# Decoder trunk on one core: adaLN halves, first up tiles and rotary tables placed elsewhere

## The chip, the cores and the metric

The kernel runs on one core of one Trainium2 chip. The metric is device time in microseconds (us) of one execution; each kernel is run several times and the median is compared. In the text PE is TensorE, DVE is VectorE, ACT is ScalarE, POOL is GpSimd and SP is SyncE. SP computes nothing here and issues most of the loads; POOL issues most of the saves and some loads.

## The reference

One layer of a decoder trunk on x of 512 tokens x 2048 channels, in float32, conditioned by a vector c through adaLN:

```python
def reference(x, c, positions, w_in, w_a, w_b, w_o, w_ada, b_ada, g_mix, g_ffn,
              w_up, conv_w, conv_b, w_down, g_final):
    c_act = jax.nn.silu(c)
    for layer in range(DEPTH):
        mod = c_act @ w_ada[layer] + b_ada[layer]
        sh1, sc1, gt1, sh2, sc2, gt2 = jnp.split(mod[:, None, :], N_MOD, axis=-1)
        h = rmsnorm(x, g_mix[layer]) * (1 + sc1) + sh1
        x = x + (1 + gt1) * mixer(h, positions, w_in[layer], w_a[layer], w_b[layer], w_o[layer])
        h = rmsnorm(x, g_ffn[layer]) * (1 + sc2) + sh2
        x = x + (1 + gt2) * conv_ffn(h, w_up[layer], conv_w[layer], conv_b[layer], w_down[layer])
    return rmsnorm(x, g_final)
```

The mixer is one input projection, a stick-breaking attention of 8 heads, a sparse attention of 8 heads with rotary positions and an indexer that picks 128 keys, two projections w_a and w_b that are merged by gates, and an output projection w_o. conv_ffn is an up-projection to 2 x 5632 channels (w_up), a causal convolution of width 3 along the tokens, silu of one half times the other, and a down-projection (w_down).

## The kernel before

**Products.** Float32 products are made of three fast ones: each operand is split into a high part and a remainder, and `mm3` (L178 to L180) multiplies high by high, high by low and low by high. Weights come into one of eight `raw` buffers of 512 KB (`load`, L154, issued by SP), ACT copies the high part to `wh` (L168) and DVE subtracts it to get `wl` (L170), in `parts`. There are three rooms for `wh` and `wl`, so weights are ready at most two products ahead of PE, and L168 waits until PE has left a room. Activations are split by `split`: ACT L197, DVE L199.

**Units.** The input projection, w_o and the up-projection are computed in `unit`: a Strassen scheme (in Winograd's form) with seven products in place of eight, each of 24 steps of 128x256. Four weight tiles a11, a21, a22, a12 are loaded, DVE makes the sums and differences of them that the products need (L268, L272, L306, L310, in place in `raw`), and others of products' results (L276, L308, L309, L312, L314). `sp` holds some of these results: L308 writes the second half of a buffer whose first half L276 wrote and reads r2, in which PE then starts the next product (T3): so PE waits for L308. A unit calls `between` at two places, where other work is put beside it. The right operands (forms of the activations) lie in `F`, a tag of 62 slots of 256 KB; 56 of them hold the forms in the up-projection, which leaves six.

**What lies beside them.** mod, the adaLN vector, is c_act times w_ada, and is made without PE: a half is a tile of w_ada, loaded into `raw` (L702, `ada_load`), times c, summed along the row by DVE (L711, `some_ada`); 96 of these halves are spread over the stages by calls of the two. They are taken in the order in which they were asked for. The last of them lie before in the units of w_o, one or two a unit, and must be done before the second norm. The rotary tables are made by a generator that runs beside the first units (`rope_tables`); ACT writes the sines (L609, L610) into a `raw` buffer of 512 KB, which is saved to memory as `rope`.

**Stages in order of time.** c and the first norm; 31 units of the input projection (w_x); indexer and values; stick-breaking heads; sparse heads with w_a beside them; w_b with the gates (L1092, L1093), which yields the operands of w_o (`y` are the heads' outputs, split at L1080); eight units of w_o, the last of them with the second norm inside (`late`, `norm_late`: its square root is L1148); the first three pairs of tiles of the up-projection, computed plainly while the second norm's operands come (`plain`, `ups`); 41 up units, each followed by its convolution, `finish` (ACT L1210 and L1217, DVE L1211, L1212 and L1219, saved to `yd` at L1220), which takes the two `w` buffers; and the down-projection (`strassen_down`) with the last norm.

**The first three pairs.** They are computed before the forms are all there. Before, the six tiles are saved to memory (`ud`) and read back one by one beside the seventh and later up units by `finish_first` (loads at L1337 into a slot, ACT L1330, DVE L1333), as the generator is run at the start of a unit.

**What sets the order.** The program is written as one sequence, and a scheduler places each instruction on its engine's queue, by what it depends on and by its place in the program. `behind` keeps an instruction after another. Within one engine, and within SP's queue of loads, the order is then fixed: what stands first must go first.

Of the kernel before, what the change touches and what calls it, by code (L numbers as in the profile page):

```python
# [36 lines left out]
NU = 3  # L37
# [39 lines left out]
def block_kernel(ctx: ExitStack, tc: tile.TileContext, A: dict, out: bass.AP):  # L77
# [164 lines left out]
    def unit(src, f, between=lambda *_: None, late=None):  # L242
# [16 lines left out]
        a11 = load(src[0], w)  # L259
        a21 = load(src[2], w)  # L260
        a22 = load(src[3], w)
        a12 = load(src[1], w)
        product(r1, parts(a11, w, True), "B11", True)
# [3 lines left out]
        s = t2k("raw", 8, w=w)  # L267
        last_v = tt(s, a21, a22, ALU.add)  # L268
# [280 lines left out]
    def rope_tables():  # L549
# [55 lines left out]
        for n, step in enumerate((64, 32)):  # L605
            o = t2k("raw", 8, w=1024)
            for i in range(P // step):
                at = slice(step * i, step * i + step)
                act(o[at, :S], q1[:step], AF.Sin, scale=TWO_PI)  # L609
                act(o[at, S:], q2[:step], AF.Sin, scale=TWO_PI if i % 2 else -TWO_PI)  # L610
                if i % 2:
                    yield
            save(rope_d[n], o)
# [134 lines left out]
    for u in range(1, 32):  # L748

        def between(i, *pins):  # L750
            if not i:
                ada_load()
            with behind(*pins):
                next(work)
                if i:
                    some_ada()

        pair = unit(A["w_x"][u - 1], f, between)
        for i, o in enumerate(pair):
            if u >= 16:  # L760
                sig = act(o, o, AF.Sigmoid)
            save(xd[2 * u + i], o)
# [114 lines left out]
    for i in range(16):  # L877
        run(fill, 2)
        run(index)
    run(fill)  # L880
# [176 lines left out]
    for hd in range(NH):  # L1057
        ada_load(2 if hd > 1 else 0)
        p, s, last = sparse_1(*pairs[hd])
        if before:  # L1060
            sparse_4(*before, y)
        if hd + 1 < NH:
            pairs.append(turned(hd + 1))
        run(fill)
        with behind(last):
            some_ada(2 if hd > 1 else 0)
        ada_load(2 if hd else 0)
        last = sparse_2(p, s)
        run(fill)
        before = hd, sparse_3(p), vb[hd // 4]  # L1070
        with behind(last):
            some_ada(2 if hd else 0)
        run(fill, 2)
    sparse_4(*before, y)
# [5 lines left out]
    y = [split(o) for o in y]  # L1080
    f = []
    merged = []
    for j in range(KT):
        t = t2k("w", 2)
        save(t, td[j])
        g = fetch(xd[33 + 2 * j])
        merged.append(g)
        ps = acc()
        w = prep(A["w_b"][j])
        for k in range(NH):  # L1090
            mm3(ps, cols(w, k), y[k], k == 0, k == NH - 1)
        tt(g, ps, g, ALU.mult)  # L1092
# [38 lines left out]
    def norm_late(c1, c2):  # L1131
# [28 lines left out]
        yield  # L1160
        tile_of(1, R)
# [15 lines left out]
    for u in range(KT // 2):  # L1177
# [6 lines left out]
        for i, c in enumerate(unit(A["w_o"][u], f, between, late)):  # L1184
# [108 lines left out]
    ud = dram("ud", 2 * NU)  # L1293
    for i, ps in enumerate(ups):
        save(ud[i], evac(ps))
# [30 lines left out]
    def finish_first():  # L1326

        def half(j, u):
            t = t2k("T", 2)
            act(t, u, AF.Identity, scale=cw[:, j, 2:3], bias=cw[:, j, 3:4])  # L1330
            for i in (1, 2):
                yield t
                stt(t[:, i:], u[:, : S - i], cw[:, j, 2 - i : 3 - i], t[:, i:], ALU.mult, ALU.add)  # L1333

        def bring(i):
            u = slot()
            nc.sync.dma_start(u, ud[i])  # L1337
            return u

        for j in range(NU):  # L1340
            u = bring(2 * j)
            yield
            yield
            for a in half(2 * j, u):
                yield
            act(a, a, AF.Silu)
            u = bring(2 * j + 1)
            yield
            yield
            for b in half(2 * j + 1, u):  # L1350
                yield
            tt(a, a, b, ALU.mult)
            save(yd[j // 2][:, j % 2 * S : (j % 2 + 1) * S], a)
            yield

    gate, first_tiles = last_gate(), finish_first()
    for j in range(NU, NJ):
        if 2 * NU <= j < 2 * NU + 2:
# [3 lines left out]
        if j >= 3 * NU:  # L1362
            run(first_tiles)
# [68 lines left out]
    def strassen_down(v, src, f, done, step=lambda i: None):  # L1432
# [12 lines left out]
        kept = []  # L1445
        for g in groups:
            a11, a21, a22 = (load(src[g, q]) for q in (0, 2, 3))
# [7 lines left out]
            kept.append(a22)  # L1455
            step(g)
# [11 lines left out]
        for i in range(2):  # L1468
            tt(c22[i], c22[i], e3[i], ALU.add)
            done((2 + i, 2 * v + 1), c22[i])  # L1470
        for g in groups:
            a12, a22 = (load(src[g, q]) for q in (1, 3))
# [3 lines left out]
            product(rc, a12, "B22", g, False)  # L1476
            step(len(groups) + g)
# [254 lines left out]
```

## Time and profile before

| what | us |
|---|---|
| median of three runs | 2738.51 |
| the three runs | 2733.37, 2738.51, 2740.41 |
| the profiled execution's own time | 2737.63 |
| its span, first to last instruction | 2735.7 |
| PE busy in it | 2677.8 |
| DVE busy | 2406.6 |
| ACT busy | 1448.4 |
| POOL busy | 315.8 |

The profile is of one execution, and busy times of engines overlap. PE's share is 98%, over 18700 matmuls; since matmuls follow each other in a pipeline, a single one lasts longer in the profile than the distance to the next. The granted clock of TensorE was 0.995 of full speed on average. DMA engines moved 202 GB/s on average. A wait is put down to the instruction or transfer that ended last before the waiting one began.

### The profile page before, as it was taken

Reading aid. Unit: us, or ns where it says so; the run is one execution under the profiler, and the core shown is the slowest. Engines: PE = TensorE matmul, PEld = TensorE weight load, DVE = VectorE, ACT = ScalarE, POOL = GpSimd, SP = SyncE. Lnnn points to the kernel's source line nnn. Section 1 sums busy time; section 2 is a strip of 40 time slices with the busy share of each in tenths; the row PEclk is TensorE's granted clock in tenths of the full one; section 3 lists DMA queues with packets and bytes.
Section 4 is the critical chain, followed back from the end, with each engine's and each line's share of the span. In section 5 each row is a group of like instructions: output and inputs, shape, how many; then the busy total and the mean of one; then the engine's idle time right before and its main releaser. Section 6 shows DMA issues by size and latency. Waiting matters only on the chain.

```text
span 2735.7 us, 47661 instructions
## 1 busy us (share of the span) xinstructions
PE 2677.8 (98%) x18700; PEld 2453.8 (90%) x18700; DVE 2406.6 (88%) x3402; ACT 1448.4 (53%) x2037; POOL 315.8 (12%) x514
## 2 busy tenths in 40 slices
PE   8999999999999999999999999999999999999998
PEld 6789999999997778889999999999999998887876
DVE  8888989999987899798878999999999997888887
ACT  4444455554446665434466555555555455546443
POOL 0000010100012211112220000000000000003011
PEclk9999999999999999999999999999999999999999
DMA  9883556666676648766864666666666436468785
GB/s 351 326 301 123 174 199 196 192 212 220 205 227 203 199 140 285 237 206 216 243 215 136 189 175 189 173 181 175 171 177 181 132 125 223 154 179 236 207 228 166
DMA packets 167853, 551.65 MB, mean 202 GB/s; under 512 B 21750, under 2 KB 22390, under 8 KB 167628
## 3 DMA queue, kind: packets, MB, share of 16 engines
q1 hardware_dynamic: 119820, 408.49, 46.4%
q0 software_dynamic: 47216, 139.73, 18.7%
q8 instruction: 147, 2.41, 0.3%
q14 instruction: 78, 0.64, 0.1%
q10 hardware_dynamic: 592, 0.39, 0.1%
HBM read 453.97 MB, written 91.14 MB: 199 GB/s over the span
## 4 chain that ended last, share of the span: by engine, by line
PE 83%; DVE 8%; DMA 4%; issue 3%; ACT 2%; SPq 0%; POOL 0%; ACTq 0%; DVEq 0%; POOLq 0%
PE att L180 13%; PE att L179 13%; PE att L178 13%; PE acc L179 12%; PE acc L180 12%; PE acc L178 12%; DVE wl L170 2%; PE acc L928 1%; DMA F<-ud 1%; ACT wh L168 1%; DMA raw<-in_w_down 1%; PE outs L179 1%; PE outs L178 1%; PE outs L180 1%; PE acc L896 1%
## 5 line engine op out<-in xcount | busy, mean ns | idle before, releaser
L168 ACT ACTIVATE wh<-raw 128x1024 fp32r<-128x1024 f32 (+1 forms) x790 | 828.8, 1055 | 945.7 <-DVE raw L272 174.9
L170 DVE TENSOR_TENSOR wl<-raw,wh 128x1024 fp32r<-128x1024 f32 (+1 forms) x790 | 953.4, 1214 | 125.3 <-ACT wh L168 117.7
L178 PE MATMUL acc<-F,wh 128*128 128x256 f32 (+1 forms) x2448 | 702.3, 287 | 9.0 <-DVE sp L308 4.3
L178 PE MATMUL att<-F,wh 128*128 128x256 f32 (+1 forms) x2448 | 704.3, 288 | 6.2 <-DVE sp L308 5.2
L180 PE MATMUL acc<-F,wl 128*128 128x256 f32 (+1 forms) x2448 | 701.5, 287 | 8.1 <-DVE wl L170 8.1
L180 PE MATMUL att<-F,wl 128*128 128x256 f32 (+1 forms) x2448 | 702.3, 287 | 4.3 <-DVE wl L170 4.3
L179 PE MATMUL att<-F,wh 128*128 128x256 f32 (+1 forms) x2448 | 701.6, 287 | 0.2 <-DVE F L199 0.2
L179 PE MATMUL acc<-F,wh 128*128 128x256 f32 (+1 forms) x2448 | 701.2, 287 | 0.1
L178 PEld LDWEIGHTS acc<-F,wh 128*128 128x128 f32 x2448 | 460.2, 188 | 21.8 <-issue 5.1
L178 PEld LDWEIGHTS att<-F,wh 128*128 128x128 f32 x2448 | 461.6, 189 | 17.4 <-issue 5.7
L180 PEld LDWEIGHTS acc<-F,wl 128*128 128x128 f32 x2448 | 460.4, 188 | 18.1 <-DVE wl L170 9.3
L180 PEld LDWEIGHTS att<-F,wl 128*128 128x128 f32 x2448 | 461.7, 189 | 13.2 <-DVE wl L170 5.0
L179 PEld LDWEIGHTS att<-F,wh 128*128 128x128 f32 x2448 | 461.7, 189 | 8.8 <-DVE F L199 0.7
L179 PEld LDWEIGHTS acc<-F,wh 128*128 128x128 f32 x2448 | 460.5, 188 | 10.1 <-DVE F L490 0.8
L178 PE MATMUL att<-wh,F 128*128 128x512 f32 x448 | 177.8, 398 | 0.2 <-ACT wh L168 0.2
L179 PE MATMUL att<-wl,F 128*128 128x512 f32 x448 | 175.3, 391 | 0.7 <-DVE wl L170 0.7
L180 PE MATMUL att<-wh,F 128*128 128x512 f32 x448 | 175.1, 391 | 0.0
L179 PE MATMUL acc<-wl,F 128*128 128x512 f32 x288 | 113.5, 394 | 4.3 <-DVE wl L170 4.3
L268 DVE TENSOR_TENSOR raw<-raw,raw 128x1024 f32<-128x1024 f32 x80 | 97.4, 1218 | 18.9 <-DMA raw<-in_w_o 14.1
L178 PE MATMUL acc<-wh,F 128*128 128x512 f32 x288 | 112.4, 393 | 0.1
L180 PE MATMUL acc<-wh,F 128*128 128x512 f32 x288 | 111.3, 391 | 0.0
L711 DVE SCALAR_TENSOR_TENSOR raw<-raw,raw 128x1024 f32<-128x1024 f32 x89 | 107.3, 1217 | 0.8 <-DMA raw<-in_w_ada 0.8
(370 smaller groups left out, 3719.9 us busy)
## 6 DMA issues: line engine op xcount, KB each, us to landing
raw<-in_w_up SPq DMA_DIRECT2D x164, 512.0 KB, 3.8
raw<-in_w_ada SPq DMA_DIRECT2D x152, 512.0 KB, 5.2
raw<-in_w_x SPq DMA_DIRECT2D x128, 512.0 KB, 4.3
raw<-in_w_down SPq DMA_DIRECT2D x104, 512.0 KB, 4.5
xd<-F POOLq DMA_DIRECT2D x64, 256.0 KB, 3.0
F<-xd POOLq DMA_DIRECT2D x64, 256.0 KB, 4.9
raw<-in_w_o SPq DMA_DIRECT2D x32, 512.0 KB, 5.5
soft<-in_w_gate SPq DMA_DIRECT2D x32, 512.0 KB, 3.9
```

What stands on the lines that cost most here:

```text
L168: pins["wh"] = act(wh, raw, AF.Copy)
L170: pins["wl"] = tt(wl, raw, wh.bitcast(F32), ALU.subtract)
L178: mm(ps, ah, bh, start=first, stop=False, skip_group_check=not check)
L179: mm(ps, ah, bl, start=False, stop=False, skip_group_check=not check)
L180: return mm(ps, al, bh, start=False, stop=last, skip_group_check=not check)
L268: last_v = tt(s, a21, a22, ALU.add)
L711: stt(w, w, 1.0, cb[half], ALU.mult, ALU.mult, accum_out=macc[:, t, half : half + 1])
L896: mm(zk, k[:, q0 : q0 + P], q[:, q0:], start=kb != 3, stop=False, skip_group_check=True)
L928: mm(o, negtri if tri else negones, i, start=False, stop=True, skip_group_check=True)
```

## The change

Seven places are edited. Line numbers in the rows are those of each kernel's own file.

1. The rotary tables are written into two slots of `F` each, in place of one `raw` buffer, and saved as two halves.
2. The adaLN halves are asked for and summed in other places: more in the 29th to 31st w_x unit, two beside the first values, three more in each of the last two sparse heads. The loop over w_o still has its calls, fewer of them, but finds nothing left.
3. The outputs of the first three sparse heads are split before the last head's end, the others after it as before.
4. The loads, the first `parts` and the first sum of w_o's first unit (`unit_head`) are written ahead of the last w_b tile's gates.
5. A square root of a constant into an unused column is written ahead of the late square root of the second norm.
6. The six first up tiles stay in their slots and are finished by `finish` just before the first, second and third up unit; the memory tensor `ud`, its saves and loads and `finish_first` are gone.
7. In `strassen_down` the loads of a group are written one group ahead.

```diff
-            o = t2k("raw", 8, w=1024)
+            o = [slot() for _ in range(2)]
...
-                act(o[at, :S], q1[:step], AF.Sin, scale=TWO_PI)
-                act(o[at, S:], q2[:step], AF.Sin, scale=TWO_PI if i % 2 else -TWO_PI)
+                act(o[0][at], q1[:step], AF.Sin, scale=TWO_PI)
+                act(o[1][at], q2[:step], AF.Sin, scale=TWO_PI if i % 2 else -TWO_PI)
...
-            save(rope_d[n], o)
+            for i in range(2):
+                save(rope_d[n][:, i * S : (i + 1) * S], o[i])
...
     for u in range(1, 32):
         def between(i, *pins):
+            free = u in (29, 30)
             if not i:
+                ada_load(2 if free else 1)
+            elif u == 29:
                 ada_load()
             with behind(*pins):
                 next(work)
-                if i:
-                    some_ada()
+                if i or u == 30:
+                    some_ada(2 if free and i else 1)
...
     for i in range(16):
+        if i in (3, 9):
+            ada_load()
         run(fill, 2)
         run(index)
+        if i in (6, 12):
+            some_ada()
...
         run(fill)
+        if hd > 5:
+            ada_load(3)
         before = hd, sparse_3(p), vb[hd // 4]
         with behind(last):
-            some_ada(2 if hd else 0)
+            some_ada((2 if hd else 0) + (3 if hd > 5 else 0))
         run(fill, 2)
+    y[:3] = [split(o) for o in y[:3]]
     sparse_4(*before, y)
...
-    y = [split(o) for o in y]
+    y[3:] = [split(o) for o in y[3:]]
...
+        if j == KT - 1:
+            head = unit_head(A["w_o"][0], KT // 2 * P)
         tt(g, ps, g, ALU.mult)
...
         with behind(*pins):
-            some_ada()
-        ada_load()
+            if i:
+                some_ada()
+        if not i:
+            ada_load()
...
         yield
+        act(r[:, 3:], eps, AF.Sqrt)
         tile_of(1, R)
...
-    ud = dram("ud", 2 * NU)
-    for i, ps in enumerate(ups):
-        save(ud[i], evac(ps))
+    ups = [evac(ps) for ps in ups]
...
-        if 2 * NU <= j < 2 * NU + 2:
+        if j < 2 * NU:
+            finish(j - NU, *ups[2 * (j - NU) : 2 * (j - NU) + 2])
+        elif j < 2 * NU + 2:
...
-        if j >= 3 * NU:
-            run(first_tiles)
         finish(j, *unit(A["w_up"][j - NU], f, beside_up))
...
+        loaded = ahead(0, 0, 2, 3)
         for g in groups:
-            a11, a21, a22 = (load(src[g, q]) for q in (0, 2, 3))
+            a11, a21, a22 = loaded
...
             kept.append(a22)
+            loaded = ahead(g + 1, 0, 2, 3)
             step(g)
```

Three places show how the order moves, all on DVE. Names end in a number of their own, and the same tile has another number in the other kernel; in the new file L268 is L281, L276 is L289, L308 is L321, L309 is L322, L711 is L725, L1211 and L1212 are L1240 and L1241, L1219 is L1248.

The first is DVE in the input projection, near 380 us, where the rotary tables are written. Before, with the first sum of the next unit (L268, of raw_3608 and raw_3610) in the last row:

```order
444 L276 TENSOR_TENSOR sp_3479<-att_3378,ta_3414 128x256
445 L711 SCALAR_TENSOR_TENSOR raw_3445,macc_68<-raw_3445,raw_92 128x1024
446 L170 TENSOR_TENSOR wl_76<-raw_3386,wh_73 128x1024
447 L170 TENSOR_TENSOR wl_83<-raw_3384,wh_79 128x1024
448 L308 TENSOR_TENSOR sp_3479<-att_3378,ta_3414 128x256
449 L309 TENSOR_TENSOR F_3508<-sp_3479,ta_3414 128x256
450 L170 TENSOR_TENSOR wl_70<-raw_3606,wh_67 128x1024
451 L312 TENSOR_TENSOR F_3507<-att_3379,sp_3479 128x256
452 L268 TENSOR_TENSOR raw_3642<-raw_3608,raw_3610 128x1024
```

And now:

```order
445 L725 SCALAR_TENSOR_TENSOR raw_3445,macc_68<-raw_3445,raw_92 128x1024
446 L281 TENSOR_TENSOR raw_3645<-raw_3611,raw_3613 128x1024
447 L170 TENSOR_TENSOR wl_76<-raw_3386,wh_73 128x1024
448 L170 TENSOR_TENSOR wl_83<-raw_3384,wh_79 128x1024
449 L321 TENSOR_TENSOR sp_3480<-att_3378,ta_3414 128x256
450 L322 TENSOR_TENSOR F_3509<-sp_3480,ta_3414 128x256
451 L170 TENSOR_TENSOR wl_70<-raw_3609,wh_67 128x1024
452 L325 TENSOR_TENSOR F_3508<-att_3379,sp_3480 128x256
453 L170 TENSOR_TENSOR wl_76<-raw_3645,wh_73 128x1024
```

The next unit's first sum (L281) has moved up, from behind that unit's first `wl` and most of the sums of results of the unit before to directly behind the adaLN half.

The second is DVE in the second and third unit of w_o. Before, from the first sum of the third unit to the results of the second:

```order
1575 L268 TENSOR_TENSOR raw_13144<-raw_13110,raw_13112 128x1024
1576 L170 TENSOR_TENSOR wl_76<-raw_12867,wh_73 128x1024
1577 L711 SCALAR_TENSOR_TENSOR raw_13006,macc_68<-raw_13006,raw_10029 128x1024
1578 L308 TENSOR_TENSOR sp_12966<-att_12861,ta_12897 128x256
1579 L309 TENSOR_TENSOR F_12995<-sp_12966,ta_12897 128x256
1580 L170 TENSOR_TENSOR wl_83<-raw_13108,wh_79 128x1024
```

And now:

```order
1582 L281 TENSOR_TENSOR raw_13167<-raw_13133,raw_13135 128x1024
1583 L170 TENSOR_TENSOR wl_83<-raw_12892,wh_79 128x1024
1584 L289 TENSOR_TENSOR sp_12992<-att_12890,ta_12926 128x256
1585 L170 TENSOR_TENSOR wl_70<-raw_12898,wh_67 128x1024
1586 L170 TENSOR_TENSOR wl_76<-raw_12896,wh_73 128x1024
1587 L321 TENSOR_TENSOR sp_12992<-att_12890,ta_12926 128x256
1588 L322 TENSOR_TENSOR F_13021<-sp_12992,ta_12926 128x256
```

The adaLN half (L711) that stood between the weights' remainders and L308 has gone; the sum of the third unit stands further up, ahead of L289. On SP's queue the loads of w_o, which had one to three loads of w_ada between units, now follow each other. The two halves L711 that stood in each of the second and later units have moved to the stages named above.

The third is DVE in the second up unit. Before, from the end of the first unit's `finish` on:

```order
1854 L1219 TENSOR_TENSOR w_15680<-w_15680,w_15685 128x512
1855 L170 TENSOR_TENSOR wl_76<-raw_15700,wh_73 128x1024
1856 L170 TENSOR_TENSOR wl_83<-raw_15694,wh_79 128x1024
1857 L310 TENSOR_TENSOR raw_15700<-raw_15700,raw_15730 128x1024
1858 L276 TENSOR_TENSOR sp_15788<-att_15692,ta_15728 128x256
1859 L268 TENSOR_TENSOR raw_15955<-raw_15921,raw_15923 128x1024
1860 L170 TENSOR_TENSOR wl_70<-raw_15700,wh_67 128x1024
1861 L170 TENSOR_TENSOR wl_76<-raw_15698,wh_73 128x1024
1862 L308 TENSOR_TENSOR sp_15788<-att_15692,ta_15728 128x256
```

And now:

```order
1860 L1248 TENSOR_TENSOR w_15684<-w_15684,w_15689 128x512
1861 L170 TENSOR_TENSOR wl_83<-raw_15709,wh_79 128x1024
1862 L1240 SCALAR_TENSOR_TENSOR w_15695<-F_15440,cw,w_15695 128x511
1863 L289 TENSOR_TENSOR sp_15803<-att_15707,ta_15743 128x256
1864 L1241 SCALAR_TENSOR_TENSOR w_15695<-F_15440,cw,w_15695 128x510
1865 L323 TENSOR_TENSOR raw_15715<-raw_15715,raw_15745 128x1024
1866 L1240 SCALAR_TENSOR_TENSOR w_15700<-F_15442,cw,w_15700 128x511
1867 L281 TENSOR_TENSOR raw_15981<-raw_15947,raw_15949 128x1024
1868 L1241 SCALAR_TENSOR_TENSOR w_15700<-F_15442,cw,w_15700 128x510
1869 L170 TENSOR_TENSOR wl_76<-raw_15713,wh_73 128x1024
1870 L1248 TENSOR_TENSOR w_15695<-w_15695,w_15700 128x512
```

Behind the first unit's `finish` (w_15684) stands the one of the second kept pair (w_15695, w_15700, from slots F_15440 and F_15442), five more instructions, spread among the sums and remainders of the second unit. The third unit holds five more in the same way. On ACT the Sqrt of the fifth edit is placed as the 64th of 1997 instructions, behind the first norm's own square root, and ACT's count of table loads is nine in both orders.

More of the change, by code (lines that the diff above doesn't have):

```diff
@@ L240, in block_kernel, with unit_head, unit @@
     units = [1]
-    def unit(src, f, between=lambda *_: None, late=None):
+    def unit_head(src, w):
+        a11, a21, a22 = (load(src[i], w) for i in (0, 2, 3))
+        first = parts(a11, w, True)
+        s = t2k("raw", 8, w=w)
+        last_v = tt(s, a21, a22, ALU.add)
+        return a11, a21, a22, load(src[1], w), first, s, last_v
+    def unit(src, f, between=lambda *_: None, late=None, head=None):
         n = len(f)
@@ L257, in product @@
             return last
[L259 to L263, printed above, removed]
+        if head:
+            a11, a21, a22, a12, first, s, last_v = head
+        else:
+            a11 = load(src[0], w)
+            a21 = load(src[2], w)
+            a22 = load(src[3], w)
+            a12 = load(src[1], w)
+            first = parts(a11, w, True)
+        product(r1, first, "B11", True)
         e = t2k("ta", 2)
@@ L266, in unit @@
         act(p1, r1, AF.Copy)
-        s = t2k("raw", 8, w=w)
-        last_v = tt(s, a21, a22, ALU.add)
+        if not head:
+            s = t2k("raw", 8, w=w)
+            last_v = tt(s, a21, a22, ALU.add)
         product(r3, parts(s, w, True), "T1", True)
@@ L1183, in block_kernel @@
         both = sb.tile([P, 10 * P], F32, tag="soft", name=nm("soft"))
-        for i, c in enumerate(unit(A["w_o"][u], f, between, late)):
+        for i, c in enumerate(unit(A["w_o"][u], f, between, late, None if u else head)):
             j = 2 * u + i
@@ L1324, in beside_up @@
             run(gate)
[L1326 to L1356, printed above, removed]
+    gate = last_gate()
     for j in range(NU, NJ):
-        if 2 * NU <= j < 2 * NU + 2:
+        if j < 2 * NU:
+            finish(j - NU, *ups[2 * (j - NU) : 2 * (j - NU) + 2])
+        elif j < 2 * NU + 2:
             x = t2k("T", 2)
@@ L1445, in strassen_down, with ahead @@
         kept = []
+        def ahead(g, *at):
+            return [load(src[g, q]) for q in at] if g in groups else None
+        loaded = ahead(0, 0, 2, 3)
         for g in groups:
-            a11, a21, a22 = (load(src[g, q]) for q in (0, 2, 3))
+            a11, a21, a22 = loaded
             product(r1, a11, "B11", g, True)
@@ L1470, in strassen_down @@
             done((2 + i, 2 * v + 1), c22[i])
+        loaded = ahead(0, 1, 3)
         for g in groups:
-            a12, a22 = (load(src[g, q]) for q in (1, 3))
+            a12, a22 = loaded
             product(r1, a12, "B21", g, False)
@@ L1476, in strassen_down @@
             product(rc, a12, "B22", g, False)
+            loaded = ahead(g + 1, 1, 3)
             step(len(groups) + g)
```

## The prediction

> **What bounds the kernel now.** I read the page first, then what TensorE (PE) waited for, then what the engines that it waited for had waited for themselves, and last windows of single stages.
>
> ```profile
> span 2735.7 us, 47661 instructions
> ...
> PE 2677.8 (98%) x18700; PEld 2453.8 (90%) x18700; DVE 2406.6 (88%) x3402; ACT 1448.4 (53%) x2037; POOL 315.8 (12%) x514
> ```
>
> PE is busy for 2677.8 of 2735.7 us, and the change keeps all its 18700 matmuls. So at most the 58 us in which PE is idle can be had, and what a slowed clock costs on top. The waits of PE (engine, tile and line, what released it: sum, times, longest):
>
> ```profile
> PE acc L180 <- DVE wl L170: 8.1, 6, 2.1
> PE outs L178 <- ACT wh L168: 6.8, 1, 6.8
> PE att L178 <- DVE sp L308: 5.2, 2, 2.9
> PE acc L179 <- DVE wl L170: 4.3, 4, 1.9
> PE acc L178 <- DVE sp L308: 4.3, 2, 3.1
> PE att L180 <- DVE wl L170: 4.3, 2, 2.1
> PE acc L352 <- DMA F<-in_c: 2.5, 1, 2.5
> PE acc L178 <- DVE F L1092: 2.4, 1, 2.4
> PE acc L178 <- ACT F L197: 1.2, 1, 1.2
> ```
>
> The 6.8 and the 2.5 are the start, which the change leaves. The rest is a few single stalls of 1 to 3 us. Within the up-projection, 1590 to 2040 us, PE waited:
>
> ```profile
> PE acc L180 <- DVE wl L170: 6.1, 4, 2.1
> PE att L180 <- DVE wl L170: 4.3, 2, 2.1
> PE att L178 <- ACT wh L168: 0.9, 2, 0.7
> ```
>
> DVE and ACT are the ones named, but what held them up there was transfers. DVE's own waits, and below them ACT's from 1560 to 2040 us:
>
> ```profile
> DVE raw L268 <- DMA raw<-in_w_o: 14.1, 5, 4.6
> DVE w L1211 <- ACT w L1210: 14.0, 6, 3.4
> ...
> DVE raw L268 <- DMA rope<-raw: 4.4, 1, 4.4
> ```
> ```profile
> ACT T L1330 <- DMA F<-ud: 25.8, 6, 5.3
> ```
>
> Three causes are seen: w_o's weights that land late, the save of a rotary table, and the reloads of the first tiles (F<-ud), for which ACT stands still six times while L168 queues behind. The windows show what follows some stalls (window and length, then busy time and count of PE, PEld, DVE, ACT, POOL, the granted clock, the DMA share, GB/s):
>
> ```profile
> 380.00:400.00 20.00, 17.48 (x140) 17.51 (x141) 17.83 (x22) 7.19 (x9) 2.16 (x4) 0.91 0.71 239
> 796.00:824.00 28.00, 28.00 (x249) 28.00 (x249) 25.46 (x34) 13.79 (x18) 1.08 (x2) 1.00 0.76 249
> 1104.70:1121.10 16.40, 16.40 (x88) 13.61 (x87) 11.54 (x27) 6.15 (x14) 2.12 (x4) 1.00 0.75 258
> 1310.00:1330.00 20.00, 17.15 (x137) 16.98 (x136) 18.36 (x22) 7.49 (x10) 4.70 (x7) 0.91 0.71 204
> 1500.00:1519.00 19.00, 19.00 (x170) 19.00 (x169) 17.81 (x22) 11.82 (x16) 1.08 (x2) 1.00 0.52 166
> 1772.90:1776.40 3.50, 3.38 (x16) 3.38 (x17) 3.50 (x5) 1.10 (x2) 0.56 (x1) 0.51 0.04 14
> 1845.00:1865.00 20.00, 17.19 (x135) 16.79 (x134) 16.29 (x20) 9.87 (x13) 1.42 (x2) 0.91 0.53 157
> 1945.00:1965.00 20.00, 18.15 (x146) 17.96 (x145) 17.45 (x22) 10.44 (x14) 1.42 (x2) 0.91 0.58 170
> ```
>
> An undisturbed up unit is the row 1500 to 1519: PE full, 170 matmuls in 19.0 us, 0.112 us each, DVE busy for 17.8 of them. After a stall the clock can fall to half: from 1772.9 us on 16 matmuls issue in 3.5 us instead of 31, so 15 x 0.112 = 1.7 us are lost besides the stall. The 0.91 in four 20-us rows (380, 1310, 1845, 1945) is the same stretch once each. These five halvings follow stalls that the change is aimed at.
>
> **The change, part by part.** The sum is made against the profiled execution's 2737.6 us (span 2735.7 and 1.9 around it); the median of the three runs is 0.9 above it.
>
> *Rotary tables.* The saves no longer hold two of the eight raw buffers, so the weight loads behind them start earlier, and L268 moves ahead on DVE. The 3.1 us stall (the longest on acc L178) and its halving go: 3.1 + 1.7 = 4.8. The slots taken are among six that the forms leave free. If the saves were late they would delay slots that nobody asks for.
>
> *adaLN halves out of the w_o units.* There L268 waited five times, 14.1 us in all, for w_o, since loads of w_ada stood ahead on SP's queue and held raw buffers; then a half (L711) stood between it and L308, for which PE waited. One such place:
>
> ```profile
> 1265.65 1.23 DVE L268 TENSOR_TENSOR raw<-raw,raw 128x1024 f32<-128x1024 f32 x1 [4.09 <-DMA raw<-in_w_o]
> 1266.80 1.22 DVE L170 TENSOR_TENSOR wl<-raw,wh 128x1024 fp32r<-128x1024 f32 x1
> 1267.93 1.22 DVE L711 SCALAR_TENSOR_TENSOR raw<-raw,raw 128x1024 f32<-128x1024 f32 x1
> ```
>
> In the new order SP has w_o's loads one behind the other, and DVE no L711 in these units. The L308 stalls go: 5.2 + (4.3 - 3.1) = 6.4, with one halving 1.7. Of the two acc L180 waits outside the up-projection (8.1 - 6.1 = 2.0) the one behind an L711 goes, 1.2; of the L1092 stall, which waits for DVE's backlog, I take 1.5 of 2.4, since one L711 of 1.2 leaves that backlog. Gain 10.8. The eleven halves go elsewhere: three into the last w_x units, two beside the values, six into the last two sparse heads. A head has DVE busy for 11.5 of 16.4 us, and three halves add 3 x 1.22 = 3.7; that fits. The w_x stretch has 25.5 of 28.0 us, and 3.7 overruns it by 1.2, some of it covered by weights prepared ahead. I take 1.5 for all of it, between 0 and 8 (the upper end: each head's three loads once waiting 4.6 us less what the 1.2 us slack takes, plus the overrun).
>
> *First three heads' outputs split early.* The 1.2 us wait for ACT F L197 goes. The work lies before, under the last head.
>
> *First w_o unit's head early, loads of the down-projection in front.* The scheduler had hoisted the former's loads already: L272, L306 and L170 stand at the same places before L1092 in both orders. Nothing. For the down-projection the order of loads changes at one place only, but near the end DVE's L170 now stands ahead of the splits L199 that it had been queued behind. From 2650 to 2680 us PE waited:
>
> ```profile
> PE acc L179 <- DVE wl L170: 2.7, 2, 1.9
> ```
>
> I take one L170's length, 1.2, of the 2.7; between -1 and 3.
>
> *Root table ahead.* The load that it is meant to move:
>
> ```profile
> L1148 ACT ACT_TABLE_LOAD  x1: 1283/1283/1283, 1397.7 to 1397.7; - x1
> ```
>
> The new Sqrt reads only a constant, and in the new order it stands among the first 70 instructions of ACT, where the root table is loaded anyway; the load in front of the late root stays. Zero, with 1.3 us as what it would have been. The Trainium skill (ScalarE: Activation LUTs, What ACT_TABLE_LOAD costs) puts a switch of sets at about 2.66 us, drain included; by it this edit, were it effective, would be worth up to that. The trace shows the 1283 ns and no drain beside it.
>
> *First tiles kept in slots.* All six F<-ud waits end, and with them 6.1 + 4.3 = 10.4 of stalls plus 0.9 of short waits for L168 just ahead of them, and three halvings, 5.1: 10.4 + 0.9 + 5.1 = 16.4. The cost: the first up unit holds one finish, where it had none (it fits), the second and third hold two. A finish costs:
>
> ```profile
> L1211 DVE SCALAR_TENSOR_TENSOR w<-F,cw,w 128x511 f32<-128x511 f32 x56 | 41.8, 746 | 14.0 <-ACT w L1210 14.0
> L1212 DVE SCALAR_TENSOR_TENSOR w<-F,cw,w 128x510 f32<-128x510 f32 x56 | 41.6, 743 | 0.0
> ...
> L1219 DVE TENSOR_TENSOR w<-w,w 128x512 f32<-128x512 f32 x28 | 19.2, 685 | 0.1
> ```
> ```profile
> L1210 ACT ACTIVATE w<-F,cw x82: 795/800/818, 1492.3 to 2282.3; 128x512 f32<-128x512 f32 x82
> ```
> ```profile
> yd<-w POOLq DMA_DIRECT2D x41, 256.0 KB, 2.3
> ```
>
> That is 2 x (0.746 + 0.743) + 0.685 = 3.7 us of DVE, so 17.8 + 3.7 = 21.5 against 19.0 of PE: 2.5 over. And there are two w buffers: the second finish's first L1210 waits until the first one's product is saved, 2.3 us, and takes 0.8, while DVE has one L170 (1.2) to do in between: about 2 us of idle DVE. So 4.5 a unit, 9 for both. Not all reaches PE, which has weights ready ahead: of ACT's 25.8 us of waits 11.3 did, 44%. 9 x 0.44 = 4; I take 5, as overload doesn't go away with one product, between 1 and 10.
>
> Sum: 4.8 + 10.8 - 1.5 + 1.2 + 0 + 1.2 + 0 + 16.4 - 5 = 27.9; 2737.6 - 27.9 = 2709.7, and I forecast **2710**.
>
> **The rivals.** *The double finish binds* (0.15). DVE is late by its full 9 us, and two halvings follow, 3.4: 12.4 instead of 5, so 2717. For it: the overload is certain. Against: six waits of ACT as long cost half.
>
> *The clock stays as it is* (0.04). If the halved stretches did not hang on these stalls, the five halvings (8.5 us) would remain: 2718. Each follows one of them, which speaks against it. The Trainium skill (TensorE: Matmul & The Clock Gate, HAM oscillation) says to leave no idle gap of PE over about 3.4 us; all stalls here are shorter, so by that rule none would halve the clock. The trace disagrees: the row at 1772.9 shows 0.51 behind a wait of 2.1.
>
> *w_o stays late* (0.12). If its loads were slow for the transfers themselves and not for the queue and the buffers, the L308 stalls and their halving stay: 8.1 more, 2718. Against: with 204 GB/s in the row at 1310 the stretch moves less than the 258 in the head.
>
> *Slower: the moved halves stall DVE* (0.03). In the last heads a half is used soon after it is asked for. If each of the eleven waited as long as the longest of w_o, 4.6, the cost is 50.6 and the time 2737.6 - 29.4 + 50.6 = 2759 (29.4 is the sum without its 1.5 for the halves). It is slower than now by what can be told, above 2746.7, from (29.4 + 9.1) / 4.6 on: nine of eleven. Against it:
>
> ```profile
> L711 DVE SCALAR_TENSOR_TENSOR raw<-raw,raw 128x1024 f32<-128x1024 f32 x89 | 107.3, 1217 | 0.8 <-DMA raw<-in_w_ada 0.8
> ```
>
> 89 halves waited for 0.8 us in all.
>
> **How the numbers follow.** The forecast has 0.66: with its costs at their ends (1 to 10, 0 to 8, -1 to 3) it runs from some 2702 to 2723, and a few us below if stalls of neighbours that I left alone go too: up to 5 more, as 2.4 and 2.7 are counted in part only and some short waits not at all. The rivals at 2717 and 2718 lie inside. Range 2697 to 2723. A measurement of this kernel can tell about 0.3%, 8.2 us: faster is below 2730.3, slower above 2746.7. Same takes a failure of two parts together (2717 plus 8 and more), 0.08; slower 0.03; faster 0.89.
>
> **What would show it.** In the new profile: no F<-ud; PE at 140 matmuls no longer in a 20-us window near 390; L268 without waits for in_w_o and no L711 from 1235 to 1330; the granted clock 1.00 except near 1400 and at both ends; L1148's table load still there; DVE full and PE short by a few us in the second and third up unit. Wrong it is if PE waits for halves in the last heads, or if the up units after the third still stall.

## The result and the profile after

The changed kernel takes 2710.85 us in the median of four runs (2709.55 to 2714.23), the kernel before 2739.19 beside it: ratio 0.9903, 95% interval 0.9885 to 0.9920. That is 28.3 us less; forecast were 2710 us and 27.9 less. Run once more, it gave 2712.48 us and 0.9915 (0.9899 to 0.9931). The profiled executions differ by 25.6 us of span.

The page's span and busy times, and the waits of PE in the new profile (line numbers are those of the new file):

```profile
span 2710.1 us, 47640 instructions
...
PE 2671.9 (99%) x18700; PEld 2449.1 (90%) x18700; DVE 2408.0 (89%) x3402; ACT 1448.6 (53%) x2038; POOL 313.7 (12%) x510
```
```profile
PE outs L178 <- ACT wh L168: 6.7, 1, 6.7
PE att L178 <- DVE sp L321: 2.6, 1, 2.6
PE acc L179 <- DVE wl L170: 2.4, 3, 1.1
PE acc L365 <- DMA F<-in_c: 2.2, 1, 2.2
PE acc L178 <- DVE F L1118: 1.9, 1, 1.9
PE acc L180 <- DVE wl L170: 1.6, 2, 0.8
PE att L179 <- DVE F L199: 1.5, 3, 1.1
PE att L178 <- ACT wh L168: 1.0, 2, 0.8
```

DVE and ACT do the same work in the same time as before. What has gone is the waiting: PE's waits for L170, 8.1 us (acc L180) and twice 4.3 (acc L179 and att L180), are 1.6, 2.4 and 0.4; the L308 waits of 5.2 and 4.3 (now L321) are one of 2.6, at a place where there was none. Windows at the places of the prediction (rotary tables; the new stall; w_o; the second and third up unit, which hold two finishes each; a later up unit):

```profile
374.00:394.00 20.00, 20.00 (x179) 20.00 (x178) 18.56 (x24) 8.25 (x10) 2.17 (x4) 1.00 0.80 267
782.20:785.70 3.50, 3.46 (x18) 3.49 (x19) 3.50 (x6) 1.30 (x2) 0.00 (x0) 0.56 0.42 70
1246.00:1343.00 97.00, 97.00 (x856) 97.00 (x855) 79.49 (x88) 50.61 (x69) 26.43 (x39) 1.00 0.73 208
1490.00:1509.00 19.00, 17.76 (x153) 17.25 (x152) 17.05 (x23) 10.46 (x15) 1.62 (x3) 1.00 0.49 173
1509.00:1528.00 19.00, 17.59 (x147) 16.85 (x147) 18.08 (x23) 11.76 (x16) 2.73 (x4) 1.00 0.50 119
1765.00:1785.00 20.00, 20.00 (x179) 20.00 (x179) 18.80 (x23) 10.99 (x14) 1.62 (x3) 1.00 0.66 176
```

PE is full through five units of w_o and where the reloads had held it up, and issues 179 matmuls near 380 us instead of 140. It is short by 17 and 23 matmuls in the two double units.

Both traces hold the same 18700 matmuls in nearly the same order, so the start of the n-th one in each shows where time was won or lost. By stage, with the forecast's terms (us, minus is faster):

| stage | matmuls | forecast | measured |
|---|---|---|---|
| start | to 510 | 0 | -1.0 |
| w_x with the rotary tables | to 5440 | -4.8 | -5.3 |
| last w_x units | to 6120 | +1.5 for all halves | +4.3 |
| values, indexer | to 6460 | (in the line above) | +1.1 |
| stick-breaking and sparse heads | to 7480 | (the same) | 0.0 |
| last head's end, split of y | to 7820 | -1.2 | -1.6 |
| w_b, w_o | to 9180 | -10.8 | -9.4 |
| second norm, plain tiles | to 10030 | 0 | +1.5 |
| first three up units | to 10710 | +5 | +5.5 |
| other up units | to 14960 | -16.4 | -19.6 |
| down-projection | to the end | -1.2 | -1.1 |
| sum | | -27.9 | -25.6 |

Two of these gains repeat in all thirteen executions profiled of the changed kernel and its variants: the w_x units with the rotary tables take 607.1 to 607.5 us (612.4 before), and the up units from the 10880th to the 14960th matmul 462.4 or 462.5 (482.0 before). The start's -1.0 is this execution's own; the other twelve lie within 0.5 us of before.

The new stall has its cause in DVE's timeline:

```profile
771.91 1.22 DVE L725 SCALAR_TENSOR_TENSOR raw<-raw,raw 128x1024 f32<-128x1024 f32 x1
773.05 0.09 DVE L725 DVE_READ_ACCUMULATOR raw<-raw,raw 128x1 f32 x1
773.05 1.22 DVE L725 SCALAR_TENSOR_TENSOR raw<-raw,raw 128x1024 f32<-128x1024 f32 x1
774.19 0.08 DVE L725 DVE_READ_ACCUMULATOR raw<-raw,raw 128x1 f32 x1
774.19 2.36 DVE L170 TENSOR_TENSOR wl<-raw,wh 128x1024 fp32r<-128x1024 f32 x2
780.53 1.22 DVE L281 TENSOR_TENSOR raw<-raw,raw 128x1024 f32<-128x1024 f32 x1 [3.98 <-DMA raw<-in_w_x]
```

Two halves (L725) give their raw buffers back at 773 and 774 us, and the weights that L281 needs land 6 us after that. It is the w_o units' old trouble, at a new place.

### The profile page after: what moved, and what is told of

Read it like the earlier page. It is cut to its first block, busy times and chain, and to the rows that moved or that the text cites. A ratio compares the mean times of both kernels' runs of the same rounds, so it can differ in the third digit from the quotient of the medians.

```text
span 2710.1 us, 47640 instructions
## 1 busy us (share of the span) xinstructions
PE 2671.9 (99%) x18700; PEld 2449.1 (90%) x18700; DVE 2408.0 (89%) x3402; ACT 1448.6 (53%) x2038; POOL 313.7 (12%) x510
## 4 chain that ended last, share of the span: by engine, by line
PE 82%; issue 6%; DVE 6%; DMA 3%; ACT 2%; POOL 1%; SPq 0%; ACTq 0%; DVEq 0%; POOLq 0%
PE att L180 13%; PE att L179 13%; PE att L178 13%; PE acc L179 12%; PE acc L180 12%; PE acc L178 12%; DVE wl L170 1%; DMA raw<-in_w_down 1%; PE outs L179 1%; PE outs L178 1%; PE outs L180 1%; PE outs L1056 1%; PE acc L949 1%; PE acc L1025 1%; DVE F L199 1%
## 5 line engine op out<-in xcount | busy, mean ns | idle before, releaser
L170 DVE TENSOR_TENSOR wl<-raw,wh 128x1024 fp32r<-128x1024 f32 (+1 forms) x790 | 952.5, 1213 | 128.8 <-ACT wh L168 119.3
L180 PE MATMUL acc<-F,wl 128*128 128x256 f32 (+1 forms) x2448 | 700.1, 286 | 1.7 <-DVE wl L170 1.6
L180 PE MATMUL att<-F,wl 128*128 128x256 f32 (+1 forms) x2448 | 700.4, 286 | 0.4 <-DVE wl L170 0.4
L179 PE MATMUL acc<-F,wh 128*128 128x256 f32 (+1 forms) x2448 | 700.3, 286 | 0.0
L179 PE MATMUL att<-F,wh 128*128 128x256 f32 (+1 forms) x2448 | 700.0, 286 | 0.2 <-DVE F L199 0.2
L180 PEld LDWEIGHTS acc<-F,wl 128*128 128x128 f32 x2448 | 459.4, 188 | 11.1 <-DVE wl L170 2.3
L179 PEld LDWEIGHTS att<-F,wh 128*128 128x128 f32 x2448 | 460.4, 188 | 8.9 <-DVE F L199 0.7
L179 PEld LDWEIGHTS acc<-F,wh 128*128 128x128 f32 x2448 | 459.6, 188 | 9.6 <-DVE F L503 0.5
L180 PEld LDWEIGHTS att<-F,wl 128*128 128x128 f32 x2448 | 460.1, 188 | 8.8 <-DVE wl L170 0.7
L179 PE MATMUL att<-wl,F 128*128 128x512 f32 x448 | 176.0, 393 | 0.2 <-DVE wl L170 0.2
L180 PE MATMUL att<-wh,F 128*128 128x512 f32 x448 | 174.5, 390 | 0.0
L179 PE MATMUL acc<-wl,F 128*128 128x512 f32 x288 | 113.3, 394 | 2.5 <-DVE wl L170 2.4
L180 PE MATMUL acc<-wh,F 128*128 128x512 f32 x288 | 111.1, 391 | 0.0
L725 DVE SCALAR_TENSOR_TENSOR raw<-raw,raw 128x1024 f32<-128x1024 f32 x89 | 106.8, 1216 | 1.0 <-DMA raw<-in_w_ada 1.0
L179 PEld LDWEIGHTS att<-wl,F 128*128 128x128 f32 x448 | 84.2, 188 | 19.7 <-issue 2.2
```

The source lines that it names most:

```text
L170: pins["wl"] = tt(wl, raw, wh.bitcast(F32), ALU.subtract)
L179: mm(ps, ah, bl, start=False, stop=False, skip_group_check=not check)
L180: return mm(ps, al, bh, start=False, stop=last, skip_group_check=not check)
L725: stt(w, w, 1.0, cb[half], ALU.mult, ALU.mult, accum_out=macc[:, t, half : half + 1])
```

## The experiments

The theory: each stall is its own, made by a transfer or a buffer, and PE gets back what is removed; the five us of the first up units are DVE's overload together with the two w buffers. The rivals: the stalls share a cause, so that a gain at one is lost at the next; or the clock's halvings, and not the stalls, make the difference. Except where a ratio stands, a number is from one profiled execution, against the changed kernel's stage of the same matmuls.

**Halves of the last w_x units moved into the sixth sparse head.**

```diff
-            free = u in (29, 30)
             if not i:
-                ada_load(2 if free else 1)
-            elif u == 29:
                 ada_load()
...
-                if i or u == 30:
-                    some_ada(2 if free and i else 1)
+                if i:
+                    some_ada()
...
-        if hd > 5:
+        if hd > 4:
             ada_load(3)
```

> The three adaLN halves that the change put into the last input-projection units go into the sixth sparse head instead; all else as in the changed kernel. Theory A (these halves hold raw buffers, so w_x loads land late, DVE waits 4.0 us for one and PE stalls 2.6 us at 782 us, followed by a halved clock): the stall and the halving near 782 us go, 4 us less, about 2707 us, and the head with three more halves shows no wait of PE. Theory B (the late load at 775 us comes from the accumulating vd saves beside it, whoever holds the buffers): the stall stays, about 2711 us. Theory C (heads are full too): the stall goes, and PE waits 1 to 4 us in the sixth head instead.

Measured: 2710.95 us. The last w_x units take 78.4 us instead of 82.6, as before the change, and the halving is gone: theory A, and not the vd saves. But the values take 1.3 more and the end of the heads 1.6 more. PE's waits from 775 to 860 us and from 1130 to 1145 us:

```profile
PE outs L829 <- DMA F<-tail: 1.7, 1, 1.7
```
```profile
PE acc L179 <- DVE F L199: 1.1, 2, 0.8
```

The wait for the split of y is back, so the stall has moved, as theory C has it, though to the heads' end and not into the sixth head. That DVE carries a backlog from that head to there is my reading; it is not shown. The other wait is one for a fetch, which a w_x that ends 4 us earlier reaches sooner. It is not the fetch alone: with no halves beside the values (the kernel with the halves back, below) w_x ends as early and PE does not wait there.

**T buffers for the kept pairs.**

```diff
-    def conv(u, j):
-        t = t2k("w", 2)
+    def conv(u, j, tag="w"):
+        t = t2k(tag, 2)
...
-            finish(j - NU, *ups[2 * (j - NU) : 2 * (j - NU) + 2])
+            finish(j - NU, *ups[2 * (j - NU) : 2 * (j - NU) + 2], tag="T")
```

> The three kept pairs are finished in buffers of another tag (T), so that they no longer share two w buffers with the units' own finishes; DVE's work is the same. If the wait for w buffers makes the 5.5 us that the changed kernel loses over the first up units (1490 to 1545 us): 2 to 3 us less, ACT's waits for the yd save there gone, about 2708 us. If it is DVE's load of 21.5 us a unit against 19.0: no change within 1 us in that stretch, about 2711 us.

**Kept pairs before every second up unit.**

```diff
-        if j < 2 * NU:
-            finish(j - NU, *ups[2 * (j - NU) : 2 * (j - NU) + 2])
-        elif j < 2 * NU + 2:
+        if j - NU in (0, 2, 4):
+            i = (j - NU) // 2
+            finish(i, *ups[2 * i : 2 * i + 2])
+        if 2 * NU <= j < 2 * NU + 2:
```

> The kept pairs are finished before the first, third and fifth up unit, so that no two units in a row hold two finishes. DVE's load as the cause: each double unit is 2.5 us over and the following one catches up, so the loss of 5.5 us over these units falls to 1 to 2, about 2707 us. The w buffers as the cause: two double units still wait for a save each, the loss stays at 4 to 5.5, about 2711 us. Slots as a new cause (four kept tiles hold slots two units longer): PE waits for L325 or ACT L317 in the second to fourth unit.

**Both together.**

> The kept pairs are finished in T buffers and before the first, third and fifth up unit. The changed kernel lost 5.5 us over the first up units, T buffers alone 2.9, the spread alone 4.9. If the 2.9 that T buffers leave are DVE's overload in two double units in a row: about 1 is left, 2707 us by the changed kernel's clock. If they are something else in the first units (the first finish lands among the last forms and the first weights): 2.5 to 3 stay.

Measured from the 10030th to the 10880th matmul, for which the kernel before, undisturbed there, needs 96.4 us: the changed kernel 101.9 (and 101.9 when run again), T buffers 99.3, spread 101.4, both 97.8. The executions took 2705.17, 2711.30 and 2705.60 us; the first and the last hold one halving each and the changed kernel's four, so the stage's times are the ones to compare. In the changed kernel ACT waits for the save of the unit's own product, and PE for what ACT has not prepared (ACT's waits from 1480 to 1530 us, then PE's to 1545):

```profile
ACT w L1239 <- DMA yd<-w: 2.1, 2, 1.7
```
```profile
PE acc L180 <- DVE wl L170: 0.8, 1, 0.8
PE att L178 <- ACT wh L168: 0.8, 1, 0.8
PE acc L178 <- ACT wh L168: 0.7, 2, 0.5
PE att L180 <- DVE wl L170: 0.4, 1, 0.4
PE acc L178 <- DVE sp L289: 0.3, 1, 0.3
```

With T buffers alone PE's waits in the same stretch are these, and no longer for ACT:

```profile
PE att L180 <- DVE wl L170: 1.6, 1, 1.6
PE acc L180 <- DVE wl L170: 0.6, 1, 0.6
```

With both (to 1590 us):

```profile
PE att L180 <- DVE wl L170: 0.5, 1, 0.5
PE outs L1140 <- DMA T<-x1d: 0.4, 1, 0.4
```

So half of the 5.5 us, 2.6, was the w buffers; spreading alone gains 0.5, as ACT still waits 4.2 us for the saves (PE waits for no slot there); and once the buffers are free, spreading gains another 1.4, which I put down to the overload. The rest of the first stall varies: the last version below, with the same two edits, had 2.0 us of it.

**The early square root held where it is of use.**

```diff
-        act(r[:, 3:], eps, AF.Sqrt)
+        with behind(pins["wh"]):
+            act(r[:, 3:], eps, AF.Sqrt)
```

> The dummy square root of the changed kernel is held behind the last weight's high part at its place in the program, so that ACT loads the root table some 7 instructions ahead of the late square root. If the table load is on the path that ends in the 2.2 us of PE waits and the halved clock near 1390 us: the late square root starts 1.3 us earlier behind its matmul, PE's waits there fall to about 1, and one or both halvings go, 1 to 4 us less, about 2708 to 2710 us. If other waits of the norm's chain end last: the load moves and PE's waits stay within 0.3 us, about 2711 us.

Measured: 2711.07 us. ACT loads the table 6 us ahead, and the late square root has none in front of it. ACT's timeline:

```profile
1382.45 1.28 ACT L1190 ACT_TABLE_LOAD   x1
1383.74 0.20 ACT L1190 ACTIVATE r<-eps 128x1 f32<-128x1 f32 x1
```

PE's waits there (1385 to 1400 us) were 0.7, 0.5 and 1.0 in the changed kernel; now:

```profile
PE acc L1263 <- DVE F L199: 1.0, 1, 1.0
PE acc L1262 <- ACT F L197: 0.5, 1, 0.5
PE outs L1182 <- DVE T L1179: 0.2, 1, 0.2
```

The stage (matmul 9180 to 9690) takes 68.7 us against 72.2 with two halvings in the changed kernel, but 69.1 in four other kernels in which the load was not moved and no halving fell there. So the table's share is 0.5 us, and 3.0 are the two halvings. PE's waits fell from 2.2 to 1.7 us, between the two cases of the expectation: of the load's 1.28 us about 0.5 reached PE, and the chain's other waits hid the rest. The Trainium skill (ScalarE: Activation LUTs, What ACT_TABLE_LOAD costs) puts a switch of sets at about 2.66 us with a drain; this trace has the load's 1.28 us and only 0.02 us between it and the activation before.

**The halves back at their places of before.**

```diff
-        if hd > 5:
-            ada_load(3)
...
         with behind(*pins):
-            if i:
-                some_ada()
-        if not i:
-            ada_load()
+            some_ada()
+        ada_load()
```

(and the calls in w_x and beside the values undone in the same way)

> Only the adaLN halves go back to their places of before (none extra in w_x, values and heads; one or two in each w_o unit); all other edits stay. If the move of the halves did what the profile of the changed kernel shows: the 2.6 us stall and the halving near 782 us go (4 less), and in the w_o units the waits of PE for L321 (6.4), for a wl behind a half (1.2) and a halving come back (8 to 9 more): 2714 to 2717 us. If the w_o stalls of before had another cause that another edit removed (the early head of the first unit): w_o stays free of them and the time falls to about 2707 us.

Measured: 2717.56 us. w_b and w_o take 191.9 us against 179.0 (188.4 before), the last w_x units 78.9 against 82.6, the values 74.6 against 75.6. PE's waits from 1205 to 1330 us are back:

```profile
PE acc L178 <- DVE F L1109: 4.9, 2, 2.7
PE att L178 <- DVE sp L321: 4.2, 2, 2.1
PE acc L180 <- DVE wl L170: 1.3, 1, 1.3
PE acc L178 <- DVE sp L321: 1.0, 1, 1.0
```

The move of the halves is what freed w_o, and no other edit. The stage is even 3.5 us longer than before, where 8 to 9 us more than the changed kernel were expected and 12.9 came: PE waits twice for the gates' product (L1109 here), 4.9 us in all against 2.4, and two halvings fall into the stage instead of one. The early head, which this kernel keeps, may have part in it: DVE waits 1.4 us at its first sum here too (see the run without it, below).

**Two weight sums held behind the last gates' product.**

```diff
+        with behind(*hold):
             tt(s, s, a11, ALU.subtract)
...
+        with behind(*hold):
             tt(a11, a11, a21, ALU.subtract)
```

(`hold` is the product L1118 in w_o's first unit, empty elsewhere)

> Two weight sums of w_o's first unit (L285 and L319 of the changed kernel, 1.2 us each) are held behind the last gates' product L1118, which stood behind them on DVE; all else as in the changed kernel. If these two are what makes PE wait 1.9 to 2.4 us for L1118 at 1228 us: that stall falls below 0.5 and the halving behind it goes, 2 to 4 us less, about 2708 us, unless the sums, now later, make PE wait in the first unit (1 to 2 us for a wl there). If L1118 is late for all the work of DVE's ahead of it: the stall stays within 0.5 us.

Measured: 2709.79 us. The wait for L1118 is gone, but PE's waits from 1225 to 1236 us are now:

```profile
PE acc L180 <- DVE wl L170: 0.8, 1, 0.8
PE acc L178 <- ACT ta L278: 0.6, 1, 0.6
PE acc L179 <- DVE F L199: 0.3, 1, 0.3
PE acc L178 <- ACT wh L168: 0.2, 1, 0.2
```

1.9 in sum, as before: DVE is late for all of it, and the order only says who waits. No halving followed in this run, and still w_b and w_o take 178.7 us against 179.0. Why DVE is late, the next run shows.

**The three edits that were forecast at nothing, or little, undone:** the early head of w_o's first unit, the square root, the down-projection's loads a group ahead.

> The early head of w_o's first unit, the early square root and the down-projection's loads a group ahead are undone; the other edits stay. If the scheduler made these places by itself, as the two orders say: within 2 us of the changed kernel, the stalls at 1228, 1390 and 2640 us as they were there. If one of them carries a gain: a new wait of PE of over 1 us in the w_b, w_o or down stage.

Measured: 2708.46 us. w_b and w_o take 176.8 us, 2.2 less than with the early head: the wait for the gates' product (L1116 in this file) is 1.0 instead of 1.9, and no halving followed. Three executions with the early head had no halving there either (T buffers with the spread, and the second and third combined kernels below), and they took 178.1 to 178.4: so the early head costs 1.3 to 1.6 us. What it does stands among DVE's waits in the changed kernel:

```profile
DVE raw L247 <- DMA raw<-in_w_o: 1.9, 1, 1.9
```

L247 is the head's first sum. It stands three instructions further up in DVE's queue than the same sum (L281) without the early head, so far up that its weights have not landed. DVE stands idle for them near 1201 us, and the rest of its order up to the gates' product, which is the same in both kernels, comes 0.9 us later against PE. In all twelve executions with the early head DVE waits there, 1.4 to 3.0 us; in this one not at all.

The norm's stage is 69.1, as elsewhere without a halving. The down-projection takes 653.6 us against 653.5 and 652.9 in the two executions of the changed kernel, but with a new wait of 1.9 us and a halving near 2629 us in it. Executions of the same code lie between 651.8 and 653.5 in that stage, so what the loads in front are worth is not shown.

**All that helped, together; first with five halves beside the values.**

```diff
-        if i in (3, 9):
+        if i in (1, 4, 7, 10, 13):
             ada_load()
...
-        if i in (6, 12):
+        if i in (3, 6, 9, 12, 15):
             some_ada()
```

(with none extra in w_x, the T buffers, the held root and the two held sums)

> Together: the three halves of the last w_x units go beside the values (five there in all, none extra in w_x), T buffers for the kept pairs, the root table held until it is of use, and the two sums behind the gates' product. If these are separate stalls, they add: 4.2 less at 782 us (0 to 1.4 given back at the values), 2.6 at the first up units, 0.8 to 4 at the late norm (halvings), 2 to 4 at 1228: 2698 to 2703 us. If a later stage takes up what an earlier one gains, as happened with the halves in a head: above 2706 us.

Measured: 2709.01 us. 4.3 us are won in the last w_x units, and the values take 79.2 us instead of 75.6, a halving included. PE's wait from 840 to 850 us:

```profile
PE outs L831 <- DMA F<-tail: 3.2, 1, 3.2
```

A second try asked for the halves only from the sixth step on, behind the weights in use, and had the T buffers with the spread and the held root:

> The three halves of the last w_x units go beside the values, asked for only from the sixth step on, behind the weights in use, so that they don't compete with the fetches that end at 846 us; T buffers and every second unit for the kept pairs; the root table held until it is of use. If it was the early loads that gave the 3.2 us wait at 846 us when all five halves stood there: 4.2 less at 782 us and nothing given back, 4 less at the first up units, 0.8 at the late norm; 2711 - 9 = 2702 us, ratio to the kernel before 0.986 to 0.988. If the stages up to 850 us are set by the fetches whatever the halves do: 2706 us.

Measured: 2707.41 us in the median, ratio 0.9897 (0.9881 to 0.9914). The values are worse, 83.2 us with two halvings. The scheduler had still placed the halves early: eight loads of w_ada are issued in the stretch below, against three in the kernel with the halves back. The wait for the tail is 4.3 us. The transfers of that stretch (812 to 850 us), with their median time to landing, are the first two lines; the third is the fetch of hd in the kernel with the halves back, in its own stretch of 808 to 843 us:

```profile
w<-hd POOLq DMA_DIRECT2D x6, 256.0 KB, 5.5
F<-tail POOLq DMA_DIRECT2D x1, 160.0 KB, 8.2
```
```profile
w<-hd POOLq DMA_DIRECT2D x6, 256.0 KB, 3.9
```

The fetches of hd go through two w buffers, one behind the other, and the tail stands behind them on POOL's queue. Each that lands 1.6 us later moves the tail: it is issued at 841.0 us here and at 835.2 us with the halves back.

**Then with the halves behind that.**

```diff
+        pins["wi"] = nc.vector.tensor_copy(...)
...
+        if i > 10:
+            with behind(pins["load"]):
+                ada_load()
...
+        if i > 12:
+            with behind(pins["wi"]):
+                some_ada()
...
+    with behind(pins["wi"]):
+        some_ada(2)
```

> As the last combined version, but the five halves beside the values are loaded behind the values' own weights and summed behind the copy that the fetch of the tail feeds (847 us), so that they can't compete with the fetches ahead of it, which made PE wait 4.3 us there; T buffers and every second unit for the kept pairs, root table held, none in the last w_x units. If that competition is the cause: no wait of PE over 1 us near 845 us, 4.2 less at 782 us kept, 4 less in the first up units, 0.8 at the late norm: 2700 to 2703 us, ratio to the kernel before 0.985 to 0.988. If the fetches end near 846 us whatever stands beside them: a wait of 4 us stays, 2705 to 2708 us.

Measured: 2702.19 us in the median (2700.99 to 2704.31), ratio to the kernel before 0.9876 (0.9860 to 0.9893). That interval lies below the one of the changed kernel when run again (0.9899 to 0.9931): this version is faster than the kernel before and than the changed kernel, though the latter's first measurement (0.9885 to 0.9920) overlaps it a little. The fetches of hd take 3.9 us to landing again, and the wait for the tail is gone. PE's waits from 775 to 900 us:

```profile
PE att L179 <- DVE wl L170: 1.6, 1, 1.6
PE att L178 <- DVE sp L321: 0.6, 1, 0.6
```

The last w_x units and the values take 155.6 us together, against 158.3 in the changed kernel and 153.0 before: about half of what the moved halves had cost there is back. At the first up unit PE waits 2.0 us. The early head is still in this version; all that helped without it was not run.

**The changed kernel again.**

> The changed kernel once more, on the same chip as its improved version: 2709 to 2714 us, ratio to the kernel before 0.990. The stalls stay where they were; whether a halving follows the one at 782 us and the ones at 1390 us can differ, 1.7 us each.

Measured: 2712.48 us, ratio 0.9915 (0.9899 to 0.9931), with every stall in place.

## Why the prediction was right

The mechanisms were right in the main: the waits that the change was aimed at went, and most terms came out one by one: the rotary tables (4.8 forecast, 5.3 measured), the split of y (1.2 and 1.6), the double finish (5 and 5.5; by the experiments 2.6 of it w buffers and 1.4, as I read it, overload; the rest is a stall where the first pair is finished) and the late square root at nothing. That the time came out within 1 us of the forecast is luck as well. Errors cancelled within the sum, the profiled executions differ by 25.6 us and not 27.9, and run again the same kernel took 2712.48 us. The down-projection (1.2 and 1.1) is no confirmation: its stage varies by more than that.

- **Halves, 1.5 forecast, 5.3 measured (4.25 and 1.05 in the two stages).** This step failed in its mechanism. I priced the last w_x units by DVE's overrun, 1.2 us. What happened is the w_o units' mechanism, which I had described just before: halves hold raw buffers, the next unit's weights are asked for late, and DVE waits 4.0 us for them. The experiment without them there gets 4.3 us back. For the two halves beside the values I worked out nothing: I did not look at the fetches that end there, for which PE now waits 0.7 us. The two heads took their six halves for nothing: the slower rival is refuted.
- **The reloads, 16.4 forecast, 19.6 measured.** Right in mechanism, too small: the stretch lost 3.2 us more around the stalls than rows and halvings show. The undisturbed rate was the better base: the kernel before needs 77.1 us for the 680 matmuls ahead of this stretch, 0.1134 us each, and measured by that rate its 4250 matmuls lost 19.1 us.
- **w_b and w_o, 10.8 and 9.4, and the early head, forecast at nothing.** The stalls in the w_o units went, all of them. The 1.5 that I took off the L1092 stall (L1118 now) came too: without the early head its 2.4 us are 1.0. But the early head, which I put at nothing because three other instructions had not moved, moved the first sum, and DVE's wait for that sum's weights brought the stall back to 1.9, with a halving behind it at 1229 us in place of the one that went at 1316 us. Without the early head the stage is 11.5 us shorter than before.
- **The norm, 0 and +1.5.** The same waits, 2.2 us, with two halvings instead of one.
- **The rivals.** The double finish did not bind beyond its term; no halving followed in those units. w_o did not stay late. That the halvings stay although the stalls go is refuted between 1410 and 2700 us, where the kernel before had three and the changed one has none. Yet a sign that I gave, a granted clock of 1.00 except near 1400 us and at both ends, did not come: halvings stand at 782 and 1229 us, each at a stall that the change made or left.

## What to carry to other kernels

Work that is moved out of a stage takes its buffers with it: ask at the new place what it asked at the old one, who waits for the buffer that it holds and which transfers stand behind its own, and not only whether the engine has time. A gain ahead of a chain of transfers is lost again at that chain, unless the chain is let through first. Work that is written earlier can come too early: its engine waits for its data, and all that stands behind it in the queue waits too. When the same instructions run in two kernels, compare the start of the n-th one: it shows each stage's gain without adding up waits.

## What the runs showed of the clock

Between the first matmuls and the end, in every one of the fourteen executions profiled, each stretch of full or halved clock in the trace lasts a whole number of times 3.413 us. A halving lasts one such step, or two. Whether one follows a stall is not set by the stall's length: the two executions of the changed kernel had waits of 2.6 and 2.8 us at the same place, and only the shorter was followed by a halving, in the row at 782.20 above. The other execution's row:

```profile
783.30:786.80 3.50, 3.48 (x30) 3.50 (x31) 3.50 (x6) 1.30 (x2) 0.00 (x0) 1.00 0.26 58
```

The Trainium skill (TensorE: Matmul & The Clock Gate, HAM oscillation) asks for no idle gap over about 3.4 us. No stall behind the start of the kernel before or of the changed one was that long, and still six halvings fell into the former's run, four into the latter's, and one to four into the others'.

The traces narrow it down. The steps can be counted on from a halving through a whole execution, so that PE's idle time (gaps over 60 ns) can be added up step by step. Away from the start (to 110 us), the end and the norm's stage, all 19 steps with 1.90 us of idle time or more, of 3.41, were followed by a halved step, and of the 16 with 1.5 to 1.9 one was. The 2.6 us at 782 us had 2.17 in one step; the 2.8 us of the other execution fell on the border of two, 0.98 and 1.84. In the norm's stage the border was lower: the eight steps with 1.52 or 1.53 us were followed by a halving, those with 1.51 or less were not. Where the steps lie against the stalls differs from execution to execution. For a reader of single runs it means that 1.7 us per halving come and go with no change in the program.
